# A hybrid decoder block on one core: a third score buffer and later transposes, one weight sum a unit, and a written order for VectorE at the start

## The chip, the core and the metric

The kernel runs on one core of a Trainium2 chip. The metric is the device time of one execution in microseconds (us). The kernel before was timed three times: 1801.48, 1805.95 and 1808.28 us, median 1805.95 us. The engines are called by the profile's names: PE (TensorE, matrix multiplications), DVE (VectorE), ACT (ScalarE), POOL (GpSimd) and SP (SyncE, which issues the DMAs). A tile in SBUF or PSUM is called by the name that it has in the program.

## What is computed

One block of a hybrid decoder in float32: 512 tokens of 2048 channels, with 16 meta tokens ahead of them (L = 528). Cut to what matters:

```python
u  = rmsnorm(concat(meta, x), norm_g)
zp = u @ w_in                       # q, k, v, g_att, z_ssm, xbc, dt, m_att, m_ssm
oa = diff_attention(q, k, v, lam)   # 8 heads; two softmax maps a head, a = p0 - lam * p1, causal, ALiBi
y_att = (rmsnorm(oa) * (1 - lam_init) * silu(g_att)) @ w_br_attn
xbc = silu(conv4(xbc) + conv_b)     # 4 taps along the tokens, 3072 channels
dtf = softplus(dt + dt_bias)
ys  = ssd_chunked(xs, dtf, -exp(a_log), bm, cm) + xs * d_skip
y_ssm = group_rmsnorm(ys * silu(z_ssm)) @ w_br_ssm
merged = sigmoid(m_att) * y_att + sigmoid(m_ssm) * y_ssm
out = rmsnorm(x + merged @ w_out, final_g)
```

## The kernel before

Every projection is a product in the Strassen-Winograd form: seven half-size products P1 to P7 a job instead of eight. A product has two units. A unit is 12 matmuls on one 128x512 piece of a weight: the weight and the token operand are each split in a high and a low part (`wh` on ACT, `wl` on DVE, L194 and L195), and three products of them are added up in one PSUM tile `d_ps`. The weights of P5, P6, P7 and P3 are sums of blocks of the weight (S1, S2 and two made in place), which DVE makes one unit at a time (L205, L208). When a product's last unit is done, its *post* on DVE or ACT adds `d_ps` to a running tile (`c`, `u`) or puts it in its place (`gth`, `sg`, `qT`, `raw`). Posts, sums and splits stand in a pipeline: sums two units ahead, splits three units ahead of the matmuls.

Beside the units run *side tasks*: generators that go one step forward at each unit. A head of the attention is such a set of tasks. `attn_rows` takes one block of 128 query rows (i = 0 to 3): scores into `s_ps`, then `biased` (DVE) writes each map's scores to a tile `sc`, ACT takes the exponentials, DVE joins the two maps in place (`cc`, then `sc<-sc,cc`, L780 to L783), PE transposes the result (`s_ps<-ident,sc`), ACT and DVE copy the transposes to `at` and `ax`, and PE multiplies with the values (`o_ps`). There are two `sc` buffers (SC = 2), so a row's two maps take both. A head takes 28 units: a job for keys and values and one for queries and the gate, qg. `attn_out` ends a head. `decays` makes the decays of the state-space part: a chain of small DVE steps ends in `dec` (L944), PE multiplies it with `tri`, and DVE goes on with `acs` and `dds`. At the same time the convolution's jobs run, whose posts fill `raw` and whose taps (`cv`, L981 and L984) are DVE's.

The order of the work: the matmuls run exactly as written, since PE is wrapped in `InOrder` (L128 is the line of all its instructions). The order on DVE, ACT and POOL is set at build time by the compiler's scheduler, by its own estimates; each engine then runs its list from first to last. Weights are loaded by SP as buffers come free, five at a time.

The stages in the trace: 0 to 62 us norm and operands; to 600 us the attention's eight heads (from 130 us in a steady rhythm); 600 to 625 us the decays; 625 to 876 us the convolution; 876 to 1310 us the state space and the gates; to 1455 us the last gate job (`ORDER_LAST`, where `oqB`, the attention's output, is also split as the next operand) and the attention's branch; then the other branch and the output.

Of the kernel before, what the change touches and what calls it, by code (L numbers as in the profile page):

```python
# [10 lines left out]
F32 = mybir.dt.float32  # L11
# [6 lines left out]
P = 128  # L18
D = 2048
S = 512  # L20
M = 16
# [28 lines left out]
ORDER_FIRST = ("P1", "P2")  # L50
ORDER_REST = ("P6", "P7", "P4", "P3", "P5")

ORDER_LAST = ("P1", "P2", "P6", "P7", "P4", "P3", "P5")


K_IN = (list(range(8)), list(range(8, 16)))
# [61 lines left out]
class InOrder:  # L118


    def __init__(self, tc, engine):
        self.tc, self.engine, self.last = tc, engine, None

    def __getattr__(self, name):
        op = getattr(self.engine, name)

        def issue(*args, **kw):
            r = op(*args, **kw)  # L128
            if self.last is not None:
                self.tc.add_manual_dep(r.ins, self.last, mybir.DependencyInfo(  # L130
                    mybir.DependencyClass.NoSync, mybir.DependencyReason.DATA), reason="in order")
            self.last = r.ins.name
            return r
        return issue
# [2 lines left out]
@with_exitstack  # L137
def block_kernel(ctx, tc, t_in, out):
    nc = tc.nc
    act, dve, pool, pe, sp = (nc.scalar, nc.vector, nc.gpsimd, InOrder(tc, nc.tensor), nc.sync)  # L140
    wd = t_in["w_all"]
    jobs = plan()

# [34 lines left out]
    def pump(most=1 << 30):  # L178
        while wstate["next"] < min(wstate["done"] + WB, n_tiles, most):
            i = wstate["next"]  # L180
            w = wp.tile([P, 1024], F32, tag="w", bufs=WB, name="w")
            sp.dma_start(w, wd[i])
            wt[i] = w
            wstate["next"] += 1
# [19 lines left out]
    def vsub(dst, a, b):  # L204
        dve.tensor_tensor(dst, a, b, ALU.subtract)  # L205

    def vadd(dst, a, b):
        dve.tensor_tensor(dst, a, b, ALU.add)  # L208
# [29 lines left out]
    def strassen(ji, width, lo, dst, fin, end=None, first=None, order=ORDER):  # L238
# [9 lines left out]
        def block(b, u):  # L248
            at = {"A11": 0, "A21": 1, "A22": 2, "A12": 3}[b] * nu + u
            return wt[tiles_of[ji][at // 2]][:, (at % 2) * 512:(at % 2 + 1) * 512]  # L250
# [4 lines left out]
        def sums(p, u):  # L255

            us = slice(u * 512, (u + 1) * 512)
            pump()
            if p == "P6":
                if u == 0:  # L260
                    parity[0] ^= 1
                    for i in range(2):
                        st[("S1", "S2")[i]] = wp.tile([P, 1024], F32, tag=("S", "So")[i ^ parity[0]], bufs=1, name="S")
                vadd(st["S1"][:, us], block("A21", u), block("A22", u))
                vsub(st["S2"][:, us], st["S1"][:, us], block("A11", u))
            elif p == "P7":
                vsub(block("A21", u), block("A11", u), block("A21", u))
            elif p == "P3":
                vsub(block("A12", u), block("A12", u), st["S2"][:, us])
# [274 lines left out]
    def token_spread(n):  # L544
        cs = slice(*((0, 3), (3, 5))[n])
        dve.tensor_tensor(s5[:, cs], ss[:, cs, 0], ss[:, cs, 1], ALU.add)
        dve.tensor_scalar(s5[:, cs], s5[:, cs], 1.0 / D, EPS, ALU.mult, ALU.add)
        pool.tensor_tensor(r5[:, cs], s5[:, cs], mhalf[:, cs], ALU.pow)
        ps = side_ps()
        for j in range(2):  # L550
            c = 2 * n + j + n
            pe.matmul(ps[:, j * P:(j + 1) * P], lhsT=r5[:, c:c + 1].to_broadcast([P, P]), rhs=ident,
                      start=True, stop=True)
        act.activation(rb[:, n, 8:], ps[:, :2 * P], AF.Copy)
        if n == 0:
            ps = side_ps()
            pe.matmul(ps[:, :M], lhsT=r5[:M, MC:MC + 1].to_broadcast([M, P]), rhs=ident[:M, :M],
                      start=True, stop=True)
            act.activation(rb[:, :, :8], ps[:, :M].rearrange("p (n t) -> p n t", n=2), AF.Copy)

    def raw(v, ks):

        g0, n = 8 * (int(v[1]) - 1), int(v[2]) - 1
        for k in range(ks.start, ks.stop):
            q = quad[v][:, k]
            dve.scalar_tensor_tensor(q, q, gn[:, g0 + k:g0 + k + 1], rb[:, n], ALU.mult, ALU.mult)
        xsplit(xv[v], quad[v][:, ks], ks)

    def x_t(v, d, p, m):
        for ks in HK:  # L570
# [108 lines left out]
    def second():  # L679
        token_spread(1)  # L680
        raw("B12", HK[0])
    dense(kv0_units[:4] + ma0[:5] + [(None, dt_tile, dt_mm)] + ma0[5:] + ma1 + kv0_units[4:8], before={
        0: begin, 1: lambda: raw("B11", HK[1]), 2: lambda: raw("B21", HK[0]), 3: lambda: raw("B21", HK[1]),
        5: lambda: token_scale(1), 8: second, 10: lambda: raw("B12", HK[1]), 11: lambda: raw("B22", HK[0]),
        13: lambda: raw("B22", HK[1]),
        15: lambda: late("T1", q11, q12, q11), 17: lambda: late("T2", q11, q22, q11),
        20: lam, 22: lambda: late("T3", q12, q22, q12)})
    late("T4", q11, q21, q11)
# [36 lines left out]
    def attn_rows(hd, i, qs, ks, kl, vt, hs):  # L725
# [56 lines left out]
        a = pr[0]  # L782
        dve.scalar_tensor_tensor(a[:, :n], pr[1][:, :n], cc, a[:, :n], ALU.mult, ALU.add)  # L783
        yield
        if i == 0:
            yield
            yield
        at = ab.tile([P, 4, P], F32, tag="at", bufs=1, name="at")
        ax = ab.tile([M, P], F32, tag="ax", bufs=1, name="ax")
        ps = side_ps()  # L790
# [12 lines left out]

    def attn_out(hd, sg, hs):

        for _ in range(4):
            yield
        sm, o_ps = hs["sm"], hs["o"]
        ssq = ab.tile([P, NT], F32, tag="ssq", bufs=2, name="ssq")
        r0 = ab.tile([P, NT], F32, tag="r0", bufs=2, name="r0")  # L810
        og = ab.tile([P, NT, P], F32, tag="at", bufs=1, name="og")
        for i in range(NT):
            act.activation(og[:, i, :], o_ps[:, i, :], AF.Square, accum_out=ssq[:, i:i + 1])
        dve.reciprocal(r0, sm[:, 0, :])
        yield
        dve.tensor_tensor(ssq, ssq, r0, ALU.mult)
        dve.tensor_tensor(ssq, ssq, r0, ALU.mult)
        dve.tensor_scalar(ssq, ssq, 1.0 / P, EPS, ALU.mult, ALU.add)  # L818
        pool.tensor_tensor(ssq, ssq, mhalf[:, :NT], ALU.pow)  # L819
        yield  # L820
        yield
        dve.tensor_tensor(r0, r0, ssq, ALU.mult)
        dve.tensor_tensor(og, o_ps, r0.unsqueeze(2).to_broadcast([P, NT, P]), ALU.mult)
        yield
        yield
        ps = side_ps()
        for i in range(NT):
            pe.transpose(ps[:, i * P:(i + 1) * P], og[:, i, :], ident)
        yield
        dve.scalar_tensor_tensor(sg, ps, gat, sg, ALU.mult, ALU.mult)  # L830
        sp.dma_start(d_oa[hd % 2, :, :, hd // 2].rearrange("t p n -> p t n"), sg.rearrange("p (t n) -> p t n", t=2))
        yield
# [10 lines left out]
        act.activation(vt[:M, 4, :], px[:M, :P], AF.Copy)  # L843
        yield

    SC = 2

    def head_tasks(hd, qT, kT, vT, vt, sg):
        hs = {}
# [55 lines left out]
    def decays(sb):  # L905
# [36 lines left out]
        act.activation(al, al, AF.Exp)  # L942
        da = e5
        dve.scalar_tensor_tensor(da, dtk, -1.0, al.unsqueeze(1).to_broadcast([P, 5, 32]), ALU.mult, ALU.mult)  # L944
        yield
        yield
        yield
# [255 lines left out]
    for v, (kh, t) in (("B11", (0, 0)), ("B12", (0, 1)), ("B21", (1, 0)), ("B22", (1, 1))):  # L1203
        oq[v] = yst.tile([P, 4, 256], F32, name=f"oq{v}")
        sp.dma_start(oq[v], d_oa[kh, t])
    name, i = rest[-1]
    dense(gate_job(name, i, d_ths, ORDER_LAST), before={6 + j: (lambda v=v: att_quarter(v))
                                            for j, v in enumerate(("B11", "B12", "B21", "B22"))})
    flush()
    tok["xv"] = xatt  # L1210
    actx.close()
# [245 lines left out]
```

## Time and profile before

| | us |
|---|---|
| median of three runs | 1805.95 |
| the profiled execution | 1807.74 |
| its span in the trace | 1806.0 |
| PE busy | 1682.2 (93%) |
| DVE busy | 1561.4 (86%) |
| ACT busy | 966.3 (54%) |
| POOL busy | 243.7 (13%) |

The span is the time from the first to the last record of the core; the execution's own time is 1.7 us longer. PE is busy for 93% of the span, so the time is best read by PE's gaps: the view of waits says which instruction PE waited for, and the timeline says where. The granted clock of PE was 0.982 of full speed in the mean; where it is 0.50 PE runs at the lower of its two levels, 1.2 instead of 2.4 GHz.

### The profile page before, as it was taken

To read this page: it belongs to the slowest core of one execution; us is meant where nothing else is said; L and a number is where in the kernel's file an instruction comes from. 1 tells how busy PE (TensorE), PEld (TensorE's weight loads), DVE (VectorE), ACT (ScalarE), POOL (GpSimd) and SP (SyncE) were. 2 spreads that over 40 slices of the span, in tenths; PEclk is the share of its full clock that TensorE was granted. 3 is DMA by queue.
4 is the path that set the end of the run, shared out by engine and by line. 5 is a ranking of instruction groups with operands and counts; after the bars stand their busy time and mean duration, and the time that the engine had idled before them with its cause. 6 is when DMAs were issued, how large, how long until landed. Compare 5 with 4: busy or idle time off the path is not lost. (4 is left out here: it accounts for less than half of the span.)

```text
span 1806.0 us, 35880 instructions
## 1 busy us (share of the span) xinstructions
PE 1682.2 (93%) x13547; PEld 1623.7 (90%) x13547; DVE 1561.4 (86%) x3013; ACT 966.3 (54%) x1960; POOL 243.7 (13%) x232
## 2 busy tenths in 40 slices
PE   3999999999999899999999999999999999989996
PEld 3998898888988899999898988989988999989996
DVE  6788888888887899999898988999987489999997
ACT  6455455554555455555646656665564244455553
POOL 0000000000000000000012222322300022223444
PEclk9999999999999999999999999999999999999998
DMA  7332222222223234333454555554467544533433
GB/s 300 107 129 64 94 79 76 76 80 84 88 73 106 92 121 139 120 126 122 157 168 150 178 159 165 168 177 146 148 206 245 186 152 152 165 127 112 145 120 105
DMA packets 136766, 244.10 MB, mean 135 GB/s; under 512 B 15089, under 2 KB 78769, under 8 KB 136081
## 3 DMA queue, kind: packets, MB, share of 16 engines
q1 hardware_dynamic: 136592, 241.81, 40.7%
q8 instruction: 107, 1.75, 0.4%
q14 instruction: 67, 0.54, 0.1%
HBM read 207.88 MB, written 33.88 MB: 134 GB/s over the span
## 5 line engine op out<-in xcount | busy, mean ns | idle before, releaser
L128 PE MATMUL d_ps<-x,wh 128*128 128x256 f32 (+1 forms) x4896 | 910.6, 286 | 17.1 <-DVE x L463 4.3
L128 PEld LDWEIGHTS d_ps<-x,wh 128*128 128x128 f32 x4896 | 761.2, 190 | 33.8 <-issue 8.8
L128 PE MATMUL d_ps<-x,wl 128*128 128x256 f32 (+1 forms) x2448 | 696.9, 285 | 17.5 <-DVE wl L195 17.2
L194 ACT ACTIVATE wh<-w 128x512 fp32r<-128x512 f32 x706 | 437.3, 627 | 408.1 <-PE d_ps L128 309.0
L128 PE MATMUL d_ps<-y,wh 128*128 128x256 f32 (+1 forms) x3216 | 600.7, 287 | 8.8 <-DVE y L463 4.7
L195 DVE TENSOR_TENSOR wl<-w,wh 128x512 fp32r<-128x512 f32 x706 | 504.9, 725 | 100.7 <-ACT wh L194 97.2
L128 PEld LDWEIGHTS d_ps<-y,wh 128*128 128x128 f32 x3216 | 498.4, 190 | 20.3 <-issue 5.7
L128 PEld LDWEIGHTS d_ps<-x,wl 128*128 128x128 f32 x2448 | 465.5, 190 | 22.7 <-DVE wl L195 22.1
L128 PE MATMUL d_ps<-y,wl 128*128 128x256 f32 (+1 forms) x1608 | 456.1, 284 | 8.6 <-DVE wl L195 8.5
L128 PEld LDWEIGHTS d_ps<-y,wl 128*128 128x128 f32 x1608 | 305.6, 190 | 10.4 <-DVE wl L195 10.4
L194 ACT ACTIVATE wh<-S 128x512 fp32r<-128x512 f32 x260 | 160.7, 628 | 184.3 <-PE d_ps L128 101.8
L195 DVE TENSOR_TENSOR wl<-S,wh 128x512 fp32r<-128x512 f32 x260 | 181.3, 712 | 30.8 <-ACT wh L194 28.4
L205 DVE TENSOR_TENSOR S<-S,w 128x512 f32<-128x512 f32 x130 | 92.7, 750 | 0.1
L205 DVE TENSOR_TENSOR w<-w 128x512 f32<-128x512 f32 x130 | 90.3, 706 | 0.0
L205 DVE TENSOR_TENSOR w<-w,S 128x512 f32<-128x512 f32 x130 | 88.9, 693 | 1.1
L208 DVE TENSOR_TENSOR S<-w 128x512 f32<-128x512 f32 x130 | 86.4, 703 | 2.2 <-DMA w<-in_w_all 2.1
L211 POOL TENSOR_TENSOR mq<-mq,cth 128x256 f32<-128x256 f32 x32 | 45.0, 1418 | 265.6 <-ACT wh L194 150.6
L819 POOL TENSOR_TENSOR ssq<-ssq,mhalf 128x4 f32<-128x4 f32 x8 | 10.5, 1308 | 483.7 <-DVE ssq L818 483.7
L1103 ACT ACTIVATE mm<-mm,acs 128x128 f32<-128x128 f32 x128 | 40.3, 389 | 36.4 <-DMA mm<-d_acs 36.4
L208 DVE TENSOR_TENSOR u<-d_ps,u 128x256 f32<-128x256 f32 (+1 forms) x130 | 54.7, 420 | 5.3 <-PE d_ps L128 4.4
L981 DVE SCALAR_TENSOR_TENSOR cv<-raw,c_conv_w,cv 128x528 f32<-128x528 f32 x72 | 53.7, 764 | 1.5 <-issue 1.1
L128 PE MATMUL s_ps<-ident,sc 128*128 128x128 f32 (+1 forms) x112 | 18.6, 283 | 31.1 <-DVE sc L783 31.1
(238 smaller groups left out, 1525.9 us busy)
## 6 DMA issues: line engine op xcount, KB each, us to landing
w<-in_w_all SPq DMA_DIRECT2D x291, 512.0 KB, 3.6
mm<-d_acs SPq DMA_DIRECT2D x16, 512.0 KB, 6.3
d_x<-cv SPq DMA_DIRECT2D x24, 264.0 KB, 2.0
q_B<-in_xT SPq DMA_DIRECT2D x8, 528.0 KB, 12.0
d_tha<-gth SPq DMA_DIRECT2D x16, 256.0 KB, 3.3
lx<-d_x SPq DMA_DIRECT2D x16, 256.0 KB, 4.5
ea<-d_acs SPq DMA_DIRECT2D x32, 128.0 KB, 3.8
d_sz<-gth SPq DMA_DIRECT2D x16, 256.0 KB, 4.0
```

The lines of the kernel that those rows point to most:

```text
L128: r = op(*args, **kw)
L194: act.activation(h[:, :n], src, AF.Copy)
L195: dve.tensor_tensor(l[:, :n], src, h[:, :n].bitcast(F32), ALU.subtract)
L205: dve.tensor_tensor(dst, a, b, ALU.subtract)
L208: dve.tensor_tensor(dst, a, b, ALU.add)
L211: pool.tensor_tensor(dst, a, b, ALU.mult)
L819: pool.tensor_tensor(ssq, ssq, mhalf[:, :NT], ALU.pow)
L981: dve.scalar_tensor_tensor(v, raw[:, j:j + L], cw[:, ft, j:j + 1], v, ALU.mult, ALU.add)
L1103: act.activation(mm[:, h, :], mm[:, h, :], AF.Relu, scale=-1.0, bias=acs[:, c, g * HPG + h:g * HPG + h + 1])
```

## The change

Six edits.

1. `SC` is 3: a third `sc` buffer.
2. Each row of the attention waits two more units between the join and the transposes (before, only row 0 did), and `attn_out` starts two units later to match.
3. `decays` waits two more units ahead of its product with `tri`.
4. S1 is summed while P1 is prepared, and S2 alone while P6 is: one weight sum a unit.
5. The last gate job takes its products in the order P1, P6, P2 instead of P1, P2, P6, and two of the four splits of `oqB` move to later units.
6. DVE is wrapped in `InOrder` until unit 13 of the first call of `dense`, so that its list there is as written (all of its instructions get L128 for a line by that). In the same place the copies of the norm's factor `rb` to SBUF go from ACT to DVE, and the low part of an operand (`x` or `y`, L463) is made one unit later than its high part.

```diff
-ORDER_LAST = ("P1", "P2", "P6", "P7", "P4", "P3", "P5")
+ORDER_LAST = ("P1", "P6", "P2", "P7", "P4", "P3", "P5")
...
-            if self.last is not None:
+            if self.last is not None and self.on:
...
-    act, dve, pool, pe, sp = (nc.scalar, nc.vector, nc.gpsimd, InOrder(tc, nc.tensor), nc.sync)
+    act, dve, pool, pe, sp = (nc.scalar, InOrder(tc, nc.vector), nc.gpsimd, InOrder(tc, nc.tensor), nc.sync)
...
+            if p == ("P1" if first is None else "P6"):
+                if u == 0:
+                    parity[0] ^= 1
+                    st["S1"] = wp.tile([P, 1024], F32, tag=("S", "So")[parity[0]], bufs=1, name="S")
+                vadd(st["S1"][:, us], block("A21", u), block("A22", u))
             if p == "P6":
                 if u == 0:
-                    parity[0] ^= 1
-                    for i in range(2):
-                        st[("S1", "S2")[i]] = wp.tile([P, 1024], F32, tag=("S", "So")[i ^ parity[0]], bufs=1, name="S")
-                vadd(st["S1"][:, us], block("A21", u), block("A22", u))
+                    st["S2"] = wp.tile([P, 1024], F32, tag=("So", "S")[parity[0]], bufs=1, name="S")
...
-        act.activation(rb[:, n, 8:], ps[:, :2 * P], AF.Copy)
+        dve.tensor_copy(rb[:, n, 8:], ps[:, :2 * P])
...
-        xsplit(xv[v], quad[v][:, ks], ks)
+        act.activation(xv[v][0][:, ks], quad[v][:, ks], AF.Copy)
+        raw_rest()
+        pieces.append((v, ks))
+
+    def raw_rest():
+        for v, ks in pieces:
+            h, l = xv[v]
+            vsub(l[:, ks], quad[v][:, ks], h[:, ks].bitcast(F32))
+        pieces.clear()
...
         raw("B12", HK[0])
+        raw("B12", HK[1])
...
         yield
-        if i == 0:
-            yield
-            yield
+        yield
+        yield
         at = ab.tile([P, 4, P], F32, tag="at", bufs=1, name="at")
...
-        for _ in range(4):
+        for _ in range(6):
             yield
...
-    SC = 2
+    SC = 3
...
         yield
+        yield
+        yield
         ps = side_ps()
         pe.matmul(ps[:, :160], lhsT=tri, rhs=da, start=True, stop=True)
...
-    dense(gate_job(name, i, d_ths, ORDER_LAST), before={6 + j: (lambda v=v: att_quarter(v))
-                                            for j, v in enumerate(("B11", "B12", "B21", "B22"))})
+    dense(gate_job(name, i, d_ths, ORDER_LAST), before={k: (lambda v=v: att_quarter(v))
+                                            for k, v in ((6, "B11"), (7, "B12"), (10, "B21"), (11, "B22"))})
```

The instructions move as follows. The first place is DVE's list in the fifth head of the attention, around the join of row 3 (`sc<-sc,cc 128x528`). `qT<-d_ps,c` is the post of the qg job's product P2, `sg` and `qT<-d_ps,u` are the posts of its P5. Before:

```order
L208 TENSOR_TENSOR qT<-d_ps,c_4623 128x256
L205 TENSOR_TENSOR S<-S,w 128x512 x2
L814 RECIPROCAL r_4933<-sm 128x4
L780 RECIPROCAL cc<-sm 128x1
L195 TENSOR_TENSOR wl<-w,wh 128x512
L781 SCALAR_TENSOR_TENSOR cc<-cc,nlam,sm 128x1
L195 TENSOR_TENSOR wl<-w,wh 128x512
L783 SCALAR_TENSOR_TENSOR sc<-sc,cc 128x528
L208 TENSOR_TENSOR u_4905<-d_ps,u_4689 128x256
```

And in the changed kernel:

```order
L128 TENSOR_TENSOR u_4897<-d_ps,u_4683 128x256
L128 TENSOR_TENSOR wl<-S,wh 128x512 x2
L128 TENSOR_TENSOR sg<-d_ps,u_4733 128x256
L128 TENSOR_TENSOR qT<-d_ps,u_4897 128x256
L128 RECIPROCAL r_4970<-sm 128x4
L128 RECIPROCAL cc<-sm 128x1
L128 SCALAR_TENSOR_TENSOR cc<-cc,nlam,sm 128x1
L128 TENSOR_TENSOR wl<-w,wh 128x512
L128 SCALAR_TENSOR_TENSOR sc<-sc,cc 128x528
```

The join stood ahead of the post of P3 (`u<-d_ps,u`); now it stands behind the two posts of P5. On PE row 3's transposes have moved to directly behind P5's last matmul.

The second place is DVE's list in the decays, from the chain's last steps to `dec`. `raw<-d_ps` are posts of the first convolution job, `cv` its taps. Before:

```order
L934 SCALAR_TENSOR_TENSOR acs<-acs,dec 128x160 x2
L936 SCALAR_TENSOR_TENSOR acs<-acs,dds 128x160
L938 SCALAR_TENSOR_TENSOR dtk<-acs,dtk 128x160
L939 COPY eac<-dtk 128x32
L940 MEMSET dtk 128x32
L941 COPY dtk<-eac 16x32
L944 SCALAR_TENSOR_TENSOR dec<-dtk,c_a_log 128x160
```

And in the changed kernel:

```order
L128 SCALAR_TENSOR_TENSOR acs<-acs,dec 128x160
L128 SCALAR_TENSOR_TENSOR cv<-raw,c_conv_w,cv 128x528 x2
L128 SCALAR_TENSOR_TENSOR acs<-acs,dds 128x160
L128 SCALAR_TENSOR_TENSOR cv<-raw,c_conv_w,cv 128x528 x2
L128 SCALAR_TENSOR_TENSOR dtk<-acs,dtk 128x160
L128 SCALAR_TENSOR_TENSOR cv<-raw,c_conv_w,cv 128x528 x2
L128 COPY eac<-dtk 128x32
L128 SCALAR_TENSOR_TENSOR cv<-cth,cv 128x528
L128 MEMSET dtk 128x32
L128 SCALAR_TENSOR_TENSOR cv<-cth,cv 128x528
L128 COPY dtk<-eac 16x32
L128 SCALAR_TENSOR_TENSOR dec<-dtk,c_a_log 128x160
```

Six taps and two gated steps of the convolution now stand between the steps of the chain. On PE the product of `dec` with `tri` stood ahead of that job's P5 and now stands behind it.

The third place is DVE's list in the last gate job, around the splits of `oqB`. Before:

```order
L195 TENSOR_TENSOR wl<-w,wh 128x512 x2
L208 TENSOR_TENSOR gth<-d_ps,c_17275 128x256
L463 TENSOR_TENSOR x<-oqB_17117,x 128x512 x2
L208 TENSOR_TENSOR u_17374<-d_ps,c_17275 128x256
L463 TENSOR_TENSOR x<-oqB_17119,x 128x512 x2
L195 TENSOR_TENSOR wl<-w,wh 128x512 x3
```

And in the changed kernel:

```order
L128 TENSOR_TENSOR u_17326<-d_ps,c_17275 128x256
L128 TENSOR_TENSOR wl<-w,wh 128x512 x4
L128 TENSOR_TENSOR gth<-d_ps,c_17275 128x256
L128 TENSOR_TENSOR x<-oqB_17117,x 128x512 x2
L128 TENSOR_TENSOR x<-oqB_17119,x 128x512 x2
L128 TENSOR_TENSOR u_17412<-d_ps,u_17326 128x256
```

P6's post (`u<-d_ps,c`) and four splits of weights now come ahead of P2's post (`gth<-d_ps,c`) instead of behind it.

## Rows read from the trace of the kernel before

**Rows 1.** The page's first part: busy us (share of the span) xinstructions

```profile
PE 1682.2 (93%) x13547; PEld 1623.7 (90%) x13547; DVE 1561.4 (86%) x3013; ACT 966.3 (54%) x1960; POOL 243.7 (13%) x232
```

**Rows 2.** Waits of PE: what for, us in total, times, longest

```profile
PE s_ps L128 <- DVE sc L783: 31.1, 23, 1.8
PE d_ps L128 <- DVE wl L195: 25.7, 25, 4.2
PE s_ps L128 <- DVE dec L944: 5.1, 1, 5.1
```

**Rows 3.** Windows by stage: busy us by engine, granted clock, DMA share, GB/s

```profile
130.00:600.00 470.00, 438.90 (x3408) 412.88 (x3407) 388.16 (x949) 253.68 (x571) 11.30 (x14) 0.99 0.25 83
625.00:876.00 251.00, 244.55 (x1990) 241.93 (x1989) 246.90 (x476) 133.95 (x227) 2.02 (x20) 1.00 0.36 122
```

**Rows 4.** PE's timeline, start: start, us, operation, [idle before <-releaser]

```profile
39.91 0.58 PE L128 MATMUL d_ps<-y,wh 128*128 128x256 f32 x1 [4.71 <-DVE y L463]
```

**Rows 5.** The timeline of DVE, and of POOL, at the start

```profile
15.95 6.55 DVE L566 SCALAR_TENSOR_TENSOR q_B<-q_B,c_norm_g,y 128x264 f32<-128x264 f32 x16
22.42 1.25 DVE L463 TENSOR_TENSOR x<-q_B,x 128x1056 fp32r<-128x1056 f32 x1
28.30 0.15 DVE L546 TENSOR_TENSOR s<-ss 128x2 f32<-128x2 f32 x1
28.73 1.09 POOL L548 TENSOR_TENSOR r<-s,mhalf 128x2 f32<-128x2 f32 x1 [15.04 <-DVE s L547]
31.93 6.56 DVE L566 SCALAR_TENSOR_TENSOR q_B<-q_B,c_norm_g,y 128x264 f32<-128x264 f32 x16 [0.43 <-ACT y L554]
```

**Rows 6.** PE's timeline in one head: transposes of rows 1, 2 and 3

```profile
272.16 0.55 PE L128 MATMUL s_ps<-ident,sc 128*128 128x128 f32 x3 [1.38 <-DVE sc L783]
280.61 0.66 PE L128 MATMUL s_ps<-ident,sc 128*128 128x128 f32 x4 [1.80 <-DVE sc L783]
292.49 0.74 PE L128 MATMUL s_ps<-ident,sc 128*128 128x128 f32 x5 [1.11 <-DVE sc L783]
```

**Rows 7.** DVE's timeline in the same head, around row 3's join

```profile
288.58 0.43 DVE L208 TENSOR_TENSOR qT<-d_ps,c 128x256 f32<-128x256 f32 x1 [0.27 <-PE d_ps L128]
288.92 0.17 DVE L814 RECIPROCAL r<-sm 128x4 f32<-128x4 f32 x1
290.98 0.69 DVE L195 TENSOR_TENSOR wl<-w,wh 128x512 fp32r<-128x512 f32 x1
291.58 0.76 DVE L783 SCALAR_TENSOR_TENSOR sc<-sc,cc 128x528 f32<-128x528 f32 x1
```

**Rows 8.** Windows after row 2's wait in two heads, and around 1342 us

```profile
224.00:228.00 4.00, 4.00 (x20) 3.52 (x19) 2.55 (x8) 1.76 (x3) 0.00 (x0) 0.59 0.38 131
280.00:284.00 4.00, 3.39 (x23) 2.95 (x24) 2.55 (x9) 1.02 (x2) 0.00 (x0) 1.00 0.41 130
1344.00:1348.00 4.00, 4.00 (x22) 4.00 (x21) 2.25 (x5) 1.31 (x3) 0.00 (x0) 0.54 0.76 245
```

**Rows 9.** PE's and DVE's timeline in the decays and the convolution

```profile
619.33 0.68 DVE L934 SCALAR_TENSOR_TENSOR acs<-acs,dec 128x160 f32<-128x160 f32 x2
621.81 0.87 PE L128 MATMUL s_ps<-dec,tri 128*128 128x160 f32 x2 [5.07 <-DVE dec L944]
628.14 0.90 DVE L208 TENSOR_TENSOR raw<-d_ps,u 128x8 f32<-128x8 f32 x4 [1.06 <-PE d_ps L128]
630.02 2.13 DVE L981 SCALAR_TENSOR_TENSOR cv<-raw,c_conv_w,cv 128x528 f32<-128x528 f32 x3 [0.38 <-ACT cv L987]
648.90 0.50 DVE L208 TENSOR_TENSOR raw<-d_ps,u 128x8 f32<-128x8 f32 x2 [0.17 <-PE d_ps L128]
```

**Rows 10.** The timeline of DVE and of PE in the last gate job

```profile
1338.57 0.42 DVE L208 TENSOR_TENSOR gth<-d_ps,c 128x256 f32<-128x256 f32 x1 [3.68 <-DMA d_ths<-gth]
1339.14 0.47 PE L128 MATMUL d_ps<-y,wh 128*128 128x256 f32 x2 [0.44 <-DVE gth L208]
1342.39 0.58 PE L128 MATMUL d_ps<-y,wl 128*128 128x256 f32 x1 [2.77 <-DVE wl L195]
```

More of the change, by code (lines that the diff above doesn't have):

```diff
@@ L121, in __init__ @@
     def __init__(self, tc, engine):
-        self.tc, self.engine, self.last = tc, engine, None
+        self.tc, self.engine, self.last, self.on = tc, engine, None, True
     def __getattr__(self, name):
@@ L558, in token_spread @@
                       start=True, stop=True)
-            act.activation(rb[:, :, :8], ps[:, :M].rearrange("p (n t) -> p n t", n=2), AF.Copy)
+            dve.tensor_copy(rb[:, :, :8], ps[:, :M].rearrange("p (n t) -> p n t", n=2))
+    pieces = []
     def raw(v, ks):
@@ L681, in second @@
         raw("B12", HK[0])
+        raw("B12", HK[1])
     dense(kv0_units[:4] + ma0[:5] + [(None, dt_tile, dt_mm)] + ma0[5:] + ma1 + kv0_units[4:8], before={
         0: begin, 1: lambda: raw("B11", HK[1]), 2: lambda: raw("B21", HK[0]), 3: lambda: raw("B21", HK[1]),
-        5: lambda: token_scale(1), 8: second, 10: lambda: raw("B12", HK[1]), 11: lambda: raw("B22", HK[0]),
-        13: lambda: raw("B22", HK[1]),
+        4: raw_rest, 5: lambda: token_scale(1), 8: second, 10: lambda: raw("B22", HK[0]), 12: lambda: raw("B22", HK[1]),
+        13: lambda: (raw_rest(), setattr(dve, "on", False)),
         15: lambda: late("T1", q11, q12, q11), 17: lambda: late("T2", q11, q22, q11),
```

## The prediction

> **What bounds the kernel now.** I read the page's busy times first: PE is busy for 93% of the span and DVE for 86% [rows 1]. So what a change is worth stands in PE's gaps, and second in places where DVE has no room. The view of PE's waits names the gaps: 31.1 us in 23 waits for the attention's join `sc`, 25.7 in 25 for weight splits `wl`, 5.1 in one for `dec` [rows 2]. The windows by stage tell where DVE could do more: in the steady attention it works 388.16 of 470 us, in the convolution 246.90 of 251 [rows 3]. In the attention DVE has spare time and only its order makes PE wait; in the convolution it has none. PE's timeline of one head shows the form of the 23 waits: row 1 of a head waits 1.38 us for its join, row 2 1.80, row 3 about 1 or less; row 0, which already has the two extra units, does not show up: eight heads with rows 1 and 2, and seven of the row-3 waits, are the 23 [rows 6]. A wait costs more than its length where PE's clock falls behind it. The windows show both: behind row 2 of one head 4 us at a granted 0.59, behind row 2 of another none below 1.00 [rows 8]; it fell in three of the eight heads. At 0.59 a window of 4 us does 2.4 us of full-speed work, so a fall costs about 1.7 us (1.64 in this row). The joins cost 31.1 + 3 x 1.7 = 36.2 us in all.
>
> **Start: 1.7 us less.** PE's restart at 39.91 hangs on a chain on DVE: the last of 16 scalings by the norm, then `y` [rows 4, 5]. The second 16 begin at 31.93, once the factor of the other token half is there: DVE makes `s` at 28.30, POOL its power from 28.73 (1.09 us), PE and a copy spread it [rows 5]. In the written order `s` stands behind 16 scalings (0.41 each, 6.55), four low parts (1.17 to 1.25) and seven splits (0.60 each, by the two starts 290.98 and 291.58 in [rows 7]): 6.6 + 4.7 + 4.2 = 15.5. They start a little before 15.95, since two splits no longer stand ahead and the copy's 0.4 comes in: from 15.6 `s` comes at 31.1, 2.8 us later than before. POOL is then done at 32.6 instead of 29.8, but before that PE was busy to 30.9 in any case and the scalings started 1.06 after; now they start at some 33.6. Yet `y` needs eight scalings instead of 16 in front of it: 33.6 + 3.3 + 1.25 = 38.2, against 39.91. I take 1.7. The best bound is 3.4, the eight scalings saved with `s` no later; the worst is 2.8 lost, `s` later and nothing saved. The early units gain nothing by themselves: the first one starts earlier, but PE waits for this chain behind them.
>
> **Attention: 5.6 us less.** With a third buffer and two more units the joins of rows 1 and 2 are done while PE runs units; their 1.38 + 1.80 = 3.18 us a head, 25.4 in all, goes. What hides it is the 2 x 1.4 us of units of PE between join and transposes. Row 3 is another matter, and here the order speaks: its transposes stand directly behind the last matmul of P5 of the qg job, and in DVE's list the join stands directly behind the two posts that need that matmul. What PE waits for is then DVE's whole stretch: two posts 0.34 each (by the starts 288.58 and 288.92), three small steps of 0.1 to 0.2, a split 0.60, the join 0.76, and two hand-overs of 0.1 to 0.15: 2.5 us [rows 7]. That is in place of about 1 or less. The ends: 2.3 with the steps at their closest, 3.1 with one more split in front. I take 2.55, near the sum: 8 x 2.55 = 20.4. For the clock rows show waits of 1.80 with a fall in three of eight, and one of 2.77 that fell, to 0.54 [rows 8, 10]. 2.55 lies nearer to the latter; I take six falls of eight, at 1.7: 10.2. Sum 30.6 against 36.2. From both sides: no fall, 20.4 (15.8 less than before); eight falls at the price of the fall after 2.77 us, 2.4, with waits of 3.1: 44 (7.8 more).
>
> The Trainium skill, "Perfetto Trace Analysis", section "Optimization Strategy", says that a gap that repeats on the engine that should be saturated can mean too few buffers for the next tile. The 23 equal waits look like that, and a third buffer is the answer to it: by the rule all 31.1 us would go, and the sum would be 30.6 us lower. This is a rival below; the rows of row 3 speak for a wait by order instead.
>
> The third buffer itself costs nothing but SBUF. The `o_ps` products and `attn_out` move with the rows; they come two units later on PE and wait for copies that have as much time as before: nothing, within 2 us either way.
>
> **Decays: 5.2 us more.** PE waits 5.07 us for `dec`, then runs the product with `tri`, then P5 [rows 9]. Now P5 (whose splits are long made) runs first, 2.9 us of work that used to lie behind the wait. If DVE's chain had kept its place the wait would shrink to 2.1. But DVE's list puts work in front of `dec` that needs P5's end: four posts (0.90 for all four [rows 9]), three splits (1.8), six taps of 0.71 (2.13 for three, 4.3), two gated steps (1.4), and in between the chain's own eight small steps, 0.24 to 0.34 for the sums, a little over 2 us together. 0.9 + 1.8 + 4.3 + 1.4 + 2.0 = 10.4, all behind P5's end. PE waits 10.3 us instead of 5.07; the clock is down after either. Does the convolution give it back, since DVE has done its taps early? DVE has no idle time from 632 us on but for 1 us, of which 0.17 is a wait for PE: the post of the next job's P5 at 648.90 [rows 9]. DVE already meets PE there with no slack; PE comes 5 us later, so DVE waits 5 us, and behind that it has no room (98% [rows 3]). So 5.2 stays. The ends: -2, if DVE's earlier taps are worth their full 5.7 less the rest, and +6, with an ACT step that the gated work waits for.
>
> **Last gate job: 5.6 us less.** P2's post `gth` needs a buffer that a store frees, and DVE stands still 3.68 us for it [rows 10]. Behind it in DVE's list were P7's and P4's splits: PE waits 0.44 and 2.77, and then runs at 0.54 and less for some 5 us, 2.4 us lost (1.84 in the full window of [rows 8], the rest ahead of it). Now P6's post and four splits stand ahead of `gth`, P2 itself ends 2.9 us later, at about 1338.7, when the store has landed, and P7 no longer needs the PSUM tile that `gth` frees. All three go: 0.44 + 2.77 + 2.4 = 5.6. At worst only 2.8 goes: the splits of `oqB` (2.5 us for four) now stand together ahead of P7's post and could make P4 wait in turn.
>
> **The sums: nothing.** S1 a unit with P1 is the same number of instructions (130 each); DVE's list has them nearly at the same places, since the scheduler had drawn them forward. From 876 us the lists agree but for the last gate job and some rows at the first state-space job: within 2 us.
>
> **The sum.** -1.7 - 5.6 + 5.2 - 5.6 = -7.7. The profiled execution took 1807.74: 1800.0. It lies 1.8 above the median of the runs shown, 1805.95, so against that 1798.
>
> **The rivals.**
> - *All waits for the join go* (the rule of the skill above would say so; the mechanism is that DVE, with spare time, gets through the posts before PE comes): 31.1 and 5.1 instead of 5.6, 1798 - 30.6 = 1767. For it: 82 us of DVE's time are free in the stage. Against: the two posts need the matmul just ahead of the transposes, no free time can change that. 0.06.
> - *PE's clock holds behind row 3's wait.* Then 20.4 and no 10.2: 1788. For it: five of eight waits of 1.80 did not fall. Against: 2.77 did, and 5.07. 0.20.
> - *Rows 1 and 2 still wait* (the change does not do what it says): if their releaser is the exponentials on ACT, which are shifted with DVE's list and not the buffer, the 25.4 stay, with row 3's 20.4 on top and one fall in each head: 45.8 + 13.6 = 59.4 instead of 30.6, 1827. It decides from the second head on. Against: in the new lists two more units of PE's matmuls stand between those joins and their transposes. 0.05.
> - *Slower: row 3's wait grows until it costs more than all that goes.* Place: the two posts of P5 in each head; price: each further split in front is 0.6 us, 4.8 over eight heads. At 4.2 us a wait and a fall in each head the joins cost 8 x 5.9 = 47 instead of 36.2, and the other terms (-2.1) no longer hold it: 1798 + 16.6 = 1815. It turns to slower than before from 3.1 us a wait. For it: before, two sums and two splits stood between the post and the join. Against: the list shows one split. 0.11.
> - *My forecast*, 1798, 0.58. Its own range is 1791 to 1806, by four to eight falls and a loss in the decays between 2 and 6.
>
> **How the numbers follow.** A change below 0.5% of 1805.95, 9.0 us, can't be told from none here, so faster is below 1796.9 and slower above 1815.0. Of the forecast's 0.58 I put 0.21 below 1796.9 and 0.37 between; with the rivals below (0.26) that is 0.47 faster. Of the two slower ones (0.16) 0.11 lies above 1815.0, 0.05 below: 0.42 the same, 0.11 slower. The range leaves out the first rival, half of the slower ones and the tails: 1785 to 1813.
>
> **What would show it.** Right: in the profile after, no waits of PE for `sc` at rows 1 and 2, eight waits of 2.3 to 3.1 us at the transposes of five blocks, windows at 0.5 to 0.6 behind most of them; one wait of about 10 us for `dec` behind P5; the wait at 1342 gone with its slow window; PE's restart at about 38. Wrong: waits for `sc` under 15 us or over 30 in all, a wait for `dec` below 7, or the convolution's stage shorter by as much as the decays are longer.

## The result and the profile after

The changed kernel took 1787.6 us in the median of four runs (1785.53 to 1792.56), the kernel before in the same set 1807.12 (1801.48 to 1809.47). The ratio is 0.990 with a 95% interval of 0.9869 to 0.9932: 1.0% faster, 19.5 us. The forecast was 1798 in a range of 1785 to 1813. The direction and the range held; the gain was nearly two and a half times the 8 us forecast, and most of it came from the attention.

The page's first part shows PE a little busier by share, with a span of 1785.9 us [rows 1].

```profile
PE 1677.5 (94%) x13547; PEld 1622.2 (91%) x13547; DVE 1556.6 (87%) x3016; ACT 962.8 (54%) x1957; POOL 243.9 (14%) x232
```

The waits of PE (what for, us in total, times, longest) answer to [rows 2]. The joins' 31.1 us in 23 waits are 17.0 in seven, and the wait for `dec` has nearly doubled.

```profile
PE d_ps L128 <- DVE wl L128: 21.4, 23, 4.3
PE s_ps L128 <- DVE sc L128: 17.0, 7, 2.6
PE s_ps L128 <- DVE dec L128: 9.8, 1, 9.8
```

PE's timeline (start, us, operation, idle time ahead and its releaser) answers to [rows 4], [rows 6] and [rows 9]. Rows 1 and 2 of the heads no longer wait at all; row 3 (five blocks) waits 2.59 us in six heads, 1.52 in the first, and not in the last.

```profile
37.88 0.58 PE L128 MATMUL d_ps<-y,wh 128*128 128x256 f32 x1 [1.16 <-DVE y L128]
...
176.13 0.76 PE L128 MATMUL s_ps<-ident,sc 128*128 128x128 f32 x5 [1.52 <-DVE sc L128]
...
286.53 1.33 PE L128 MATMUL s_ps<-ident,sc 128*128 128x128 f32 x5 [2.59 <-DVE sc L128]
...
342.49 0.76 PE L128 MATMUL s_ps<-ident,sc 128*128 128x128 f32 x5 [2.58 <-DVE sc L128]
...
610.14 0.87 PE L128 MATMUL s_ps<-dec,tri 128*128 128x160 f32 x2 [9.76 <-DVE dec L128]
```

DVE's timeline shows the three places: the factor at the start and the scalings behind it, the stretch from P5's posts to row 3's join, the taps ahead of `dec`, and the post `gth` of the last gate job. They answer to [rows 5, 7, 9, 10].

```profile
30.79 0.16 DVE L128 TENSOR_TENSOR s<-ss 128x2 f32<-128x2 f32 x1
33.27 3.31 DVE L128 SCALAR_TENSOR_TENSOR q_B<-q_B,c_norm_g,y 128x264 f32<-128x264 f32 x8
...
283.98 0.42 DVE L128 TENSOR_TENSOR sg<-d_ps,u 128x256 f32<-128x256 f32 x1
284.33 0.41 DVE L128 TENSOR_TENSOR qT<-d_ps,u 128x256 f32<-128x256 f32 x1
...
285.11 0.69 DVE L128 TENSOR_TENSOR wl<-w,wh 128x512 fp32r<-128x512 f32 x1
285.71 0.76 DVE L128 SCALAR_TENSOR_TENSOR sc<-sc,cc 128x528 f32<-128x528 f32 x1
...
606.69 1.45 DVE L128 SCALAR_TENSOR_TENSOR cv<-raw,c_conv_w,cv 128x528 f32<-128x528 f32 x2
...
609.67 0.33 DVE L128 SCALAR_TENSOR_TENSOR dec<-dtk,c_a_log 128x160 f32<-128x160 f32 x1
...
1322.45 0.42 DVE L128 TENSOR_TENSOR gth<-d_ps,c 128x256 f32<-128x256 f32 x1 [0.21 <-DMA d_ths<-gth]
```

The windows (busy us of each engine, granted clock, DMA share, GB/s) behind two of the equal waits of row 3 answer to [rows 8]: the clock fell behind one and not behind the other.

```profile
286.00:290.00 4.00, 3.47 (x17) 3.39 (x18) 2.38 (x5) 1.15 (x2) 0.00 (x0) 0.57 0.00 0
342.00:346.00 4.00, 3.51 (x29) 3.49 (x30) 2.96 (x6) 1.74 (x3) 0.00 (x0) 1.00 0.00 0
```

Where the 20.1 us between the two spans lie can be read by fixed places, which are the same instructions of PE in both profiles. PE's restart on `y` comes 2.0 us earlier (39.91, now 37.88), but at 78.91 us of the kernel before PE is only 1.0 ahead (now 77.91): in between the granted clock was 0.92 in the mean, and 0.95 before. From there to 595.98 us, when the last head is done, the changed kernel needs 18.3 us less, and that is the attention's gain:

```profile
78.91:595.98 517.07, 485.97 (x3803) 459.95 (x3802) 426.51 (x1016) 280.72 (x619) 13.15 (x16) 0.99 0.26 87
77.91:576.72 498.81, 481.77 (x3803) 459.28 (x3802) 421.11 (x1016) 276.61 (x617) 10.63 (x16) 0.99 0.28 90
```

PE's idle time in it falls from 31.1 to 17.0 us, and its busy time by 4.2. Of the 19.3 us at that place the longer wait for `dec` gives back 4.7. In the last gate job (from 1317 to 1374 us before) the two profiles differ by another 5.9 us, of which more below. The rest is unchanged within 1 us.

One pair of profiles can mislead, since the clock's falls differ from one execution to the next. Over all profiles of this document that have the old or the new form of a stretch (the number in brackets), the means are:

| stretch, us of the kernel before | with the old work | with the new work | difference |
|---|---|---|---|
| start to 78.91: when PE gets there | 79.2 (four) | 77.1 (ten) | -2.1 |
| attention, 78.91 to 595.98 | 518.8 (three) | 498.3 (five) | -20.5 |
| decays to state space, to 1317.35 | 719.3 (three) | 726.3 (seven) | +7.0 |
| last gate job and what follows, to 1374.34 | 55.1 (three) | 52.0 (eleven) | -3.1 |

They add up to -18.7, where the medians differ by 19.5.

### The profile page after: what moved, and what is told of

It is laid out like the page before. It is cut to its first block, busy times and chain, and to the rows that moved or that the text cites. A ratio compares the mean times of both kernels' runs of the same rounds, so it can differ in the third digit from the quotient of the medians.

```text
span 1785.9 us, 35840 instructions
## 1 busy us (share of the span) xinstructions
PE 1677.5 (94%) x13547; PEld 1622.2 (91%) x13547; DVE 1556.6 (87%) x3016; ACT 962.8 (54%) x1957; POOL 243.9 (14%) x232
## 5 line engine op out<-in xcount | busy, mean ns | idle before, releaser
L128 PE MATMUL d_ps<-x,wh 128*128 128x256 f32 (+1 forms) x4896 | 912.9, 287 | 15.1 <-DVE cth L128 4.3
L128 PEld LDWEIGHTS d_ps<-x,wh 128*128 128x128 f32 x4896 | 764.4, 191 | 31.9 <-issue 9.3
L128 PE MATMUL d_ps<-x,wl 128*128 128x256 f32 (+1 forms) x2448 | 698.6, 285 | 17.0 <-DVE wl L128 16.5
L128 PE MATMUL d_ps<-y,wh 128*128 128x256 f32 (+1 forms) x3216 | 600.0, 286 | 9.1 <-ACT wh L194 4.6
L128 DVE TENSOR_TENSOR wl<-w,wh 128x512 fp32r<-128x512 f32 x706 | 505.4, 727 | 105.1 <-ACT wh L194 99.6
L128 PEld LDWEIGHTS d_ps<-y,wh 128*128 128x128 f32 x3216 | 498.1, 190 | 20.3 <-issue 5.5
L128 PEld LDWEIGHTS d_ps<-x,wl 128*128 128x128 f32 x2448 | 464.9, 190 | 22.5 <-DVE wl L128 22.0
L128 PE MATMUL d_ps<-y,wl 128*128 128x256 f32 (+1 forms) x1608 | 455.7, 283 | 4.9 <-DVE wl L128 4.9
L128 PEld LDWEIGHTS d_ps<-y,wl 128*128 128x128 f32 x1608 | 303.9, 189 | 6.3 <-DVE wl L128 6.3
L128 DVE TENSOR_TENSOR wl<-S,wh 128x512 fp32r<-128x512 f32 x260 | 182.9, 719 | 26.8 <-ACT wh L194 24.7
L128 DVE TENSOR_TENSOR S<-S,w 128x512 f32<-128x512 f32 x130 | 93.2, 753 | 0.0
L128 DVE TENSOR_TENSOR w<-w 128x512 f32<-128x512 f32 x130 | 90.8, 715 | 0.0
L128 DVE TENSOR_TENSOR w<-w,S 128x512 f32<-128x512 f32 x130 | 89.4, 699 | 0.9
L128 DVE TENSOR_TENSOR S<-w 128x512 f32<-128x512 f32 x130 | 86.3, 705 | 2.1 <-DMA w<-in_w_all 2.0
L128 DVE TENSOR_TENSOR u<-d_ps,u 128x256 f32<-128x256 f32 (+1 forms) x130 | 55.2, 424 | 9.3 <-PE d_ps L128 8.8
L128 DVE SCALAR_TENSOR_TENSOR cv<-raw,c_conv_w,cv 128x528 f32<-128x528 f32 x72 | 54.5, 779 | 1.1 <-issue 0.7
L211 POOL TENSOR_TENSOR state<-state,dec 128x512 f32<-128x512 f32 x12 | 19.6, 1630 | 172.3 <-DVE state L128 172.2
```

Of the source, the lines that this page charges most:

```text
L211: pool.tensor_tensor(dst, a, b, ALU.mult)
```

## The experiments

The theory was that the attention's gain comes from PE having work between join and transposes, that row 3's wait is DVE's stretch behind P5's posts, that the later product with `tri` costs 5 us, and that the last gate job is 6 us better by its order. Each experiment names its rival. Seven are the changed kernel with one edit undone or one more made, two run the kernel before, and three put several edits on top of the change. Times are medians. Ratios are to the kernel before in the same set, and are not the quotients of the medians; its median was 1806.2 to 1808.6 us in the three sets, so a difference between medians of two sets can be off by some 2 us.

**The decays as before.** Two units less ahead of the product with `tri`:

```diff
-        yield
-        yield
         ps = side_ps()
         pe.matmul(ps[:, :160], lhsT=tri, rhs=da, start=True, stop=True)
```

> The changed kernel without edit 3: the product with tri stands two units earlier again, ahead of P5. Theory A (the later product costs 5 us, since DVE's list puts the convolution's first taps ahead of dec and the convolution has no slack to give it back): the wait for dec falls from 9.8 to about 5 us, and everything behind it lies 4.5 to 5 us earlier: some 1783. Rival B (the taps done early are given back in the convolution): the wait falls by the same, but the end stays within 1 us of 1787.6.

Measured: 1782.79 us, ratio 0.9865 (0.9831 to 0.9899). The waits of PE have

```profile
PE s_ps L128 <- DVE dec L128: 5.4, 1, 5.4
```

The wait fell by 4.4 us and the median by 4.8: what is done early on DVE was not given back. Theory A, though the interval overlaps that of the changed kernel; the same edit is made once more below, on top of another, and gains there too.

**The third buffer alone.** The two extra units of rows 1 to 3 undone:

```diff
         yield
-        yield
-        yield
+        if i == 0:
+            yield
+            yield
         at = ab.tile([P, 4, P], F32, tag="at", bufs=1, name="at")
...
-        for _ in range(6):
+        for _ in range(4):
```

> The changed kernel without edit 2: three sc buffers, but rows 1 to 3 again go from the join to the transposes without the two extra units. Theory A (the units do it: PE has work between the join and the transposes): waits for sc are back at about 31 us in 23, and the time is 15 to 18 us longer than the changed kernel, some 1804. Rival B (the buffer does it: rows 1 and 2 waited for a buffer): waits for sc stay near 17 us or below and the time stays at 1788 or goes below it, since row 3 then waits 1 us instead of 2.6.

Measured: 1811.68 us, ratio 1.0015 (0.9991 to 1.0040), 24 us longer than the changed kernel. Neither theory's waits came: they are fewer than before and more than 17, but the attention is no faster. The waits, one timeline row of seven, and the windows of the stage and behind that row:

```profile
PE s_ps L128 <- DVE sc L128: 23.9, 14, 2.4
```

```profile
275.31 1.12 PE L128 MATMUL s_ps<-ident,sc 128*128 128x128 f32 x4 [2.40 <-DVE sc L128]
```

```profile
130.00:600.00 470.00, 446.05 (x3350) 419.06 (x3349) 382.99 (x935) 247.55 (x560) 11.28 (x14) 0.95 0.25 82
276.00:280.00 4.00, 4.00 (x17) 3.53 (x16) 1.07 (x5) 0.49 (x1) 0.00 (x0) 0.50 0.31 119
```

Row 1's waits are gone by the buffer alone; row 2's grew from 1.80 to 2.40, and behind all seven waits of 2.40 the clock went to 0.50. The granted clock of the whole stage is 0.95 against 0.99 [rows 3]. So the buffer alone does not make the gain, and in this execution the 7 us of waits that it saved went back into a slower clock. It was one of the longer ones, 1815.12 us at a granted clock of 0.971 in the mean; the twelve executions lie between 1797.8 and 1817.3, and the four at 0.976 or more took 1797.8 to 1804.4. (The times of this kernel also hold what the later decays cost and the start gains.)

**Two buffers.** The units without the third buffer:

```diff
-    SC = 3
+    SC = 2
```

> The changed kernel with two sc buffers: the two extra units without the third buffer. Theory A (the buffer is needed for the units: with two, the next row's second map can't be written to sc until the transposes have read the row before, so the wait moves from the transposes to the next scores): waits of PE in the attention are 15 us or more above the 17.0 of the changed kernel, and the time is 1800 or longer. Rival B (the units alone do it): the same 17 us or less of waits, within 3 us of 1787.6; in this list row 3's join stands ahead of P5's posts, so that its wait of 2.6 could go too, and then it would be 1770 to 1775.

Measured: 1815.85 us, ratio 1.0049 (1.0034 to 1.0064). The waits for `sc` are gone, and another has come:

```profile
PE s_ps L128 <- DVE mn L128: 29.7, 8, 4.0
```

Row 2's transposes wait 3.68 us a head for the next row's scores to leave PSUM, which they do through a `sc` buffer that is not free. Theory A: units and buffer belong together, and either alone is no faster than before. Row 3's wait is gone here as well: in this kernel's list on DVE its join stands ahead of P5's posts again, and well ahead of its transposes (230.16 and 236.02 us in one head).

**Row 3 two units later still**, on top of the change:

```diff
         yield
         yield
+        if i == 3:
+            yield
+            yield
         at = ab.tile([P, 4, P], F32, tag="at", bufs=1, name="at")
...
-        for _ in range(6):
+        for _ in range(8):
```

> The changed kernel with two more units between join and transposes in row 3 alone (and the head's output two units later). Theory A (row 3's 2.6 us are DVE's stretch from P5's posts to the join, and 2.9 us of PE's work in front of the transposes cover it): the six or seven waits of 2.6 go, 17 us, and with the two falls of the clock 20: some 1768. Rival B (PE then waits for something that comes later in the head, the copies or the output of the head before, or the next head's scores for an s_ps tile): another wait of 1 to 3 us a head takes its place and the time stays above 1780.

Measured: 1767.47 us, ratio 0.9783 (0.9756 to 0.9810). No wait for a join is left in the attention, and none has come in its place. Between the same two places as above PE is busy without a gap and at full clock:

```profile
76.50:554.08 477.58, 477.58 (x3802) 456.46 (x3801) 420.03 (x1015) 276.29 (x618) 9.90 (x10) 1.00 0.28 94
```

Theory A: the medians differ by 20.1 us, and 17.0 us of waits and two falls of the clock at 1.7 were 20.4.

**The last gate job's order as before.**

```diff
-ORDER_LAST = ("P1", "P6", "P2", "P7", "P4", "P3", "P5")
+ORDER_LAST = ("P1", "P2", "P6", "P7", "P4", "P3", "P5")
...
-                                            for k, v in ((6, "B11"), (7, "B12"), (10, "B21"), (11, "B22"))})
+                                            for j, v in enumerate(("B11", "B12", "B21", "B22"))})
```

> The changed kernel without edit 5: the last gate job again in the order P1, P2, P6, with the four splits of oqB at four units in a row. Theory A (the order alone freed the 0.44 and 2.77 us and the slow window behind them): both waits are back and the time is 6 us longer than the changed kernel, some 1793.5. Rival B (the gain there comes with the earlier arrival of the whole stage, the store having landed): the stage stays as it is, 1787.6.

Measured: 1787.21 us, ratio 0.9887 (0.9867 to 0.9907): no difference that the times show. DVE waited less for the store than in the kernel before, and PE for one split:

```profile
1316.13 0.42 DVE L128 TENSOR_TENSOR gth<-d_ps,c 128x256 f32<-128x256 f32 x1 [1.21 <-DMA d_ths<-gth]
```

```profile
1319.94 0.39 PE L128 MATMUL d_ps<-y,wl 128*128 128x256 f32 x1 [0.97 <-DVE wl L128]
```

Rival B, by the time. Two more runs took this up.

**The last order alone**, edit 5 and nothing else in the kernel before:

```diff
-ORDER_LAST = ("P1", "P2", "P6", "P7", "P4", "P3", "P5")
+ORDER_LAST = ("P1", "P6", "P2", "P7", "P4", "P3", "P5")
...
-                                            for j, v in enumerate(("B11", "B12", "B21", "B22"))})
+                                            for k, v in ((6, "B11"), (7, "B12"), (10, "B21"), (11, "B22"))})
```

> The kernel before with edit 5 alone: the last gate job in the order P1, P6, P2, two splits of oqB later. Theory A (the order is worth its 6 us in the kernel before as well): 6 us less than before, some 1801. Rival B (how long VectorE stands there hangs on when the store lands behind a burst of loads, 1.2 us in one execution and 3.7 in another, and the order is worth only what that costs PE in an execution): 0 to 2 us less than before, within the measurement's noise.

Measured: 1805.85 us, ratio 0.9994 (0.9979 to 1.0009). DVE still waits, PE does not:

```profile
1336.81 0.42 DVE L208 TENSOR_TENSOR gth<-d_ps,c 128x256 f32<-128x256 f32 x1 [0.98 <-DMA d_ths<-gth]
```

**The kernel before again.** Nothing is edited.

> The kernel before, unchanged, a second profile: how long VectorE waits for the store in the last gate job, and PE behind it. Theory A: 3.7 us again, PE 0.44 and 2.77. Rival B: another length, 1 to 3 us, and PE waits 1 us or none.

Measured: 1809.03 us in one run. The store's wait and PE's behind it:

```profile
1337.93 0.42 DVE L208 TENSOR_TENSOR gth<-d_ps,c 128x256 f32<-128x256 f32 x1 [2.54 <-DMA d_ths<-gth]
```

```profile
1341.75 0.39 PE L128 MATMUL d_ps<-y,wl 128*128 128x256 f32 x1 [2.31 <-DVE wl L195]
```

With the old order DVE waited 3.68, 2.54 and 1.21 us in three executions and PE 3.2, 2.3 and 1.0. In the eleven profiles with the new order PE has no such wait. The order ends it, but how much of it is kept is open. The stretch took 57.0, 55.7 and 52.7 us with the old order and 50.7 to 54.5 with the new, 3.1 less in the mean; PE waits later in it for `cth`, 1.2 to 3.0 us with the new order. The times can't show a gain of that size: alone the order gave 0.9994, and the interval reaches from 3.8 us less to 1.6 more. So the 6 us of the pair of profiles are in part what one execution of the kernel before happened to lose. Rival B, as to the time.

**The start as before.** VectorE's list from the scheduler, the copies on ACT, the low part with the high part:

```diff
-    act, dve, pool, pe, sp = (nc.scalar, InOrder(tc, nc.vector), nc.gpsimd, InOrder(tc, nc.tensor), nc.sync)
+    act, dve, pool, pe, sp = (nc.scalar, nc.vector, nc.gpsimd, InOrder(tc, nc.tensor), nc.sync)
...
-        dve.tensor_copy(rb[:, n, 8:], ps[:, :2 * P])
+        act.activation(rb[:, n, 8:], ps[:, :2 * P], AF.Copy)
...
-        act.activation(xv[v][0][:, ks], quad[v][:, ks], AF.Copy)
-        raw_rest()
-        pieces.append((v, ks))
+        xsplit(xv[v], quad[v][:, ks], ks)
...
```

> The changed kernel without edit 6: VectorE's list at the start is the scheduler's, the copies of rb are on ACT again and an operand's low part is made with its high part. Theory A: PE's restart on the second operand goes from 37.9 back to 39.9 us, and the time is 2 us longer, some 1789.6; nothing else moves. Rival B (the written order also set what comes after unit 13, so the attention's lists change): more than 4 us either way, with waits for sc other than the 17.0 us of the changed kernel.

Measured: 1791.05 us, ratio 0.9897 (0.9871 to 0.9924). PE's restart is back at 39.91 us and the waits for `sc` are the same 17.0. The median is 3.4 longer, but the interval overlaps the changed kernel's; the 2 us are read from the profiles, not from the times. The four profiles with the old start get to the place at 78.91 us at 78.9 to 79.8, the ten with the new one at 76.5 to 77.9. Theory A.

**The sums as before.** S1 and S2 both with P6:

```diff
-            if p == ("P1" if first is None else "P6"):
+            if p == "P6":
                 if u == 0:
                     parity[0] ^= 1
-                    st["S1"] = wp.tile([P, 1024], F32, tag=("S", "So")[parity[0]], bufs=1, name="S")
+                    for i in range(2):
+                        st[("S1", "S2")[i]] = wp.tile([P, 1024], F32, tag=("S", "So")[i ^ parity[0]], bufs=1, name="S")
...
```

> The changed kernel without edit 4: S1 and S2 are both summed while P6 is prepared. Theory A (the scheduler had drawn the sums forward anyway, so the lists are nearly the same): within 2 us of 1787.6. Rival B (part of the attention's 17 us comes from the sums: S1 away from row 3's join): more waits for sc or wl and 3 to 8 us longer.

Measured: 1788.30 us, ratio 0.9892 (0.9873 to 0.9910), with the same 17.0 us for `sc`. Theory A: the edit is worth nothing that can be measured.

**Row 3 and the decays later.** The version with row 3 later, and eight more units ahead of the product with `tri`:

```diff
-        yield
-        yield
-        yield
-        yield
-        yield
+        for _ in range(13):
+            yield
         ps = side_ps()
         pe.matmul(ps[:, :160], lhsT=tri, rhs=da, start=True, stop=True)
```

> The kernel with two more units in row 3, and the product with tri another eight units later, in the convolution's second job. Theory A (PE's wait for dec is only a matter of place, and the convolution, where VectorE has next to no free time, then starts without the hole that VectorE has while it waits for that product): the wait of 9.8 us goes, with the slow window of some 2 us behind it, and of these 12 us at least half is kept to the end: 1756 to 1762. Rival B (the convolution is VectorE's: what PE does not wait for dec it waits for wl): waits for wl grow by 5 us or more in the convolution, and the time stays at 1764 to 1768.

Measured: 1764.64 us, ratio 0.9755 (0.9733 to 0.9777). Both were wrong on the wait, which neither went nor turned into waits for `wl` (6.9 us of them in the stretch of the convolution, 7.1 without the later product); the time is rival B's:

```profile
PE s_ps L128 <- DVE dec L128: 7.5, 1, 7.5
```

The scheduler moved the chain's steps back with the product: on DVE they stand apart, between posts, sums, splits and taps, and `dec` comes at 596.80 us with no idle time on DVE ahead of it. `dec` is late because DVE's list makes it late.

**Row 3 later, the decays as before:**

```diff
+        if i == 3:
+            yield
+            yield
         at = ab.tile([P, 4, P], F32, tag="at", bufs=1, name="at")
...
-        for _ in range(6):
+        for _ in range(8):
...
-        yield
-        yield
         ps = side_ps()
         pe.matmul(ps[:, :160], lhsT=tri, rhs=da, start=True, stop=True)
```

> The two gains found so far together: two more units in row 3 (1767.5 by itself) and the product with tri as in the kernel before (4.8 us by itself). Theory A (they lie in different stages and add): 1762 to 1764. Rival B (the convolution, which has no free time on VectorE, takes part of it back): 1766 or more.

Measured: 1758.43 us, ratio 0.9736 (0.9715 to 0.9757): 9 us less than row 3 alone, where 3.5 to 5.5 were expected. They add at least. The rest may be the clock, of which there is one profile each: from the end of the attention to the last gate job 0.99 was granted here and 0.98 with row 3 alone.

**Row 3 later, the decays written.** Row 3 is as in the version above, and DVE keeps the written order from the start of the decays to `dec`:

```diff
         dve.memset(x5, 0.0)
         yield
+        dve.on = True
         ps = side_ps()
...
-        yield
-        yield
-        yield
-        yield
-        yield
+        dve.on = False
+        for _ in range(13):
+            yield
         ps = side_ps()
         pe.matmul(ps[:, :160], lhsT=tri, rhs=da, start=True, stop=True)
```

> Two more units in row 3, VectorE's list as written from the start of the decays to dec, and the product with tri eight units later than in the changed kernel: dec then stands where nothing waits for it. Theory A (the wait for dec goes whole, and VectorE no longer stands still behind that product either): no wait for dec, 1756 to 1761. Rival B (with no wait for dec PE is ahead and waits for wl instead, since the convolution is bound by VectorE): waits for wl in the convolution grow by 3 us or more, and the time is no better than 1762.

Measured: 1753.58 us, ratio 0.9705 (0.9684 to 0.9726): 3% faster than the kernel before, 34 us less than the changed one. Row 3 and decays later, above, differs from it by the written order alone: the medians are 11 us apart, by the ratios 9, and the wait of 7.5 us for `dec` is gone here. The 251 us over the convolution, which now begin at 578, show DVE busy for 249.89, against 246.90 [rows 3]:

```profile
578.00:829.00 251.00, 242.95 (x1985) 240.36 (x1985) 249.89 (x489) 134.15 (x229) 2.01 (x20) 1.00 0.37 124
```

PE waits 10.5 us for `wl` in twelve waits from the end of the attention to the first state-space job, 3 to 4 us more than in the changed kernel, so part of the saved wait did turn into waits for DVE, as rival B had it; the time is theory A's.

## Why the prediction was right, and where its sizes were off

**The start** was right: forecast -1.7, measured -2.0 at the restart, and -2.1 at 78.91 us in the mean of the profiles (-1.0 in the pair). The chain came as worked out, `s` at 30.79 (31.1 forecast), the scalings at 33.27 (33.6), `y` 1.25 us behind eight of them.

**The attention** had the right mechanism and the wrong size: -5.6 forecast, -18.3 measured. Rows 1 and 2 lost their waits as said; in six heads row 3 waits for exactly the stretch that was laid out, 2.59 us where 2.55 was taken. What failed is "I take six falls of eight, at 1.7: 10.2". The changed kernel's profile has two falls in six waits of 2.59, and with the four variants that have the same waits nine in 30: 3.4 us in place of 10.2. The second size is the number of waits: seven with 17.0 us in place of eight with 20.4, since the first head waits 1.52 and the last none. These two are 10.2 of the 12.7 us. The third is a term that the sum put at nothing: a wait costs PE a little beyond its length and its fall. Less the falls at 1.7, PE is busy for 480.9 us in the stretch with 23 waits, 478.4 with seven, and 477.6 with none: an estimated 0.11 to 0.16 us a wait, 2.5 us for the 16 that went. (The prediction also calls the 23 waits equal; they have three lengths [rows 6].)

The kernel lies nearest to the rival in which the clock holds, given 0.20, and not to the forecast. That the rival's 1788 was met so closely is in part luck: the clock did fall twice, and the missing eighth wait and PE's shorter busy time made up for it; and its sum holds the last gate job's 5.6 as well, which the times do not show. The forecast's own range, 1791 to 1806, was missed, and the wider one held by 2.6 us.

One thing beside DVE's stretch was not in the prediction. The small steps ahead of the join also need the sums that ACT makes with row 3's exponentials, and the second of these was done at 284.55 us, 0.11 ahead of the first small step:

```profile
284.37 0.18 ACT L789 ACTIVATION_READ_ACCUMULATOR sc<-sc,mn 128x1 f32 x1
284.66 0.17 DVE L128 RECIPROCAL r<-sm 128x4 f32<-128x4 f32 x1
```

It is 0.1 us in all six heads. So, as far as this profile tells, with P5's posts out of the way the join would have come hardly earlier unless the exponentials did too. No run tried that; later transposes cover both.

**That all joins' waits go** (the rule of the Trainium skill, "Perfetto Trace Analysis", section "Optimization Strategy", taken alone) did not happen: 17.0 us were left in the changed kernel, and 23.9 where the buffer came alone (1811.7 us). The traces agree with the rule so far as the buffer is needed: without it the two units gave 1815.9. Row 3's part went when its transposes were written later.

**That rows 1 and 2 still wait**, and **that row 3's wait grows to 4 us**, did not come; 2.59 is far from the 3.1 at which the second one would have turned.

**The decays** were right: +5.2 forecast, a wait of 10.3; measured +4.7 in the wait of 9.76, +7.0 over the stretch to the last gate job in the mean of the profiles, and 4.8 in the median when it was undone. That the convolution gives nothing back was right as well.

**The last gate job** was too large as a term. The profile after shows PE's waits of 0.44 and 2.77 us gone as forecast, but undoing the edit changed no time, and alone it gave 0.9994. The step that failed is the first sentence on it: the 3.68 us at the store were taken for the kernel's, and they were one execution's; the next had 2.54, and the falls of the clock behind them differ as well. The sum counted 5.6 us where the profiles have 3.1 in the mean and the times show none.

**The sums** were right: nothing forecast, nothing measured.

## What to carry to other kernels

When a wait ends on an instruction that stands in its engine's list behind work that needs the matmul just ahead of the waiting one, a buffer alone does not help: here the consumer had to be written later on the waiting engine, with enough buffers for that distance; one without the other gained nothing. An engine whose order a scheduler sets will drift with every consumer that is moved (`dec` came later both times that its product did), so where a short chain matters its order should be written, which was worth some 10 us here. A term that rests on how long one DMA took in one profile needs a second profile before it enters a sum.

## What the runs showed of the hardware that was not expected

Whether PE's clock falls at a wait is not set by the wait's length alone. At row 2's transposes it fell in 13 of 24 waits of 1.80 us (three executions of kernels with the old attention), in seven of seven of 2.40 and eight of eight of 3.67 to 4.01 (one execution each). At row 3's it fell in nine of 30 of 2.59 us (five executions). A fall took about 1.7 us at row 3 and more where it stayed at 0.50 (the window above at 276 us). What tells the two places apart was not tried and stays open. The number of falls differs between executions of one kernel, three and six in the attention in the two profiles of the kernel before, which at 1.7 us each is an estimated 5 us between the two.
